# One transfer for three tiles of x, gamma first at the start, and a newly laid order of work, in an RMSNorm + QKV product on one core

## The chip, the core and the metric

The kernel runs on one core of a Trainium2 chip. A core has TensorE (PE, matrix products into PSUM), VectorE (DVE), ScalarE (ACT) and GpSimd (POOL, which doesn't touch PSUM here), and SyncE (SP), which here issues all transfers but that of gamma. The metric is the time of one execution on the device, in microseconds (us). Before the change the median of three runs is 361.82 us (358.01 to 362.8).

## The reference

```
batch, n_heads, seq, head_dim = 8, 12, 1024, 64       # dim = 768
x: (8, 1024, 768) float32; gamma: (768,); w_qkv: (768, 2304) float32
rms = np.sqrt(np.mean(x ** 2, axis=-1, keepdims=True) + eps)
x_norm = x / rms * gamma
return np.matmul(x_norm, w_qkv).astype(np.float32)    # (8, 1024, 2304)
```

x is 8192 rows of 768, which is 64 tiles of 128 rows. The result has 2304 columns.

## The kernel before, in words

**Tiles.** The columns of the result are halved, c = 0 and 1, 1152 columns each (HW), and each half has three blocks of 384 columns (CW). The depth of 768 is six slices of 128 (KO), halved into three and three (H). gamma is multiplied into the weights once (conv, into w_b), and the row's 1/rms is multiplied into x or into the result.

**Head.** The first 7 tiles of x (N_HEAD) are computed plainly while the weights still arrive: load_x, cast to bf16, tr (six transposes on TensorE), cp out of PSUM, then mm, one matmul of 128 x 384 for each depth slice (L517 to L521). evac multiplies by 1/rms on the way out of PSUM, store_h stores.

**Triples.** The other 57 tiles go in 19 groups of three, g = 0 to 18. Three tiles by two depth halves, times two depth halves by three column blocks, would be 18 block products; the kernel does it in 15 by sums and differences of blocks. For the weights these sums are made once per half (quad scales a block to f16 by a bound on it, bsum adds; 15 + 3 forms). For x they are made in each triple by osum (11 sums, nearly all on GpSimd). The tables A_OF, B_OF and CHAIN say which sums are multiplied (L361 to L364), and the 15 products accumulate in two PSUM banks (chains 0 and 1) whose value is read between the products. A triple passes through these steps:

- load_t (L577): one tile of x from HBM into one third of a buffer XI (three buffers); one DMA for each tile, 393 KB
- pstat (L582), prms (L585) on ScalarE: sum of squares of each tile, then the square root for three; precip (L588) on VectorE: the reciprocals
- pcast (L591): the tile times 1/rms, to f16
- pxbar (L601): the three tiles turned by one DMA transpose
- osum (L615): the 11 sums
- product (L619): three matmuls of 128 x 384 each, 0.163 us apart; 15 for each half of the columns
- hold (L632): the first value of a result block, moved from PSUM to the output buffer times a scale, on ScalarE
- join (L635): the further values, added to or subtracted from what lies in an output buffer, on VectorE
- pstore (L639): a finished 128 x 1152 piece to HBM, 590 KB. There are 14 output buffers (OUT): 8 of their own, and 6 that lie in w_b once the weights are used up (the profile names those w_b). An argument at the end of hold is the buffer that is taken.

**Order.** The order of the work is written out by hand in the string PLAN: items "name engine arguments" apart by ";", run through once in that order. Each engine does its items strictly in their order, and so does SyncE with its DMAs; an item waits for the data and buffers that it needs, and what stands behind it on the same engine waits too. So a DMA whose data isn't ready holds up all later DMAs. The products of two halves, and of neighbouring triples, are interleaved so that TensorE has work while one chain's value is read.

**Start.** TensorE first runs 14 matmuls on zeros (idle, L479). Then come the transposes of the first tile and of gamma (gamma_tr, L483), and behind the cast of the third tile VectorE copies gamma out of PSUM (gamma_cp, L487), for which the conversion of the weights waits.

Of the kernel before, what the change touches and what calls it, by code (L numbers as in the profile page):

```python
# [10 lines left out]
load_x SP 0 0;load_w SP 0 0 6;load_x SP 1;load_w SP 0 1 7;idle PE 14 512 0;load_x SP 2;load_w SP 0 2 8;load_w SP 0 3 9;  # L11
cast ACT 0 0;load_w SP 0 4 10;stat ACT 0;load_w SP 0 5 11;recip DVE 0;cast ACT 1;load_x SP 3 1;stat ACT 1;load_x SP 4;
tr PE 0 1;gamma_tr PE 2;recip DVE 1;cp ACT 0 0;tr PE 1 3;load_x SP 5;cast DVE 2;gamma_cp DVE;stat ACT 2;tr PE 2 4;cp DVE 1;
conv POOL 0 0 0 1;load_w SP 1 0 12;conv DVE 0 0 1 3;conv POOL 0 1 0 3;mm PE 0 0 0 5;mm PE 1 0 0 6;cp ACT 2;conv DVE 0 2 0 3;
mm PE 0 1 0 7;mm PE 1 1 0 1;mm PE 0 2 0 2;load_w SP 1 1 13;mm PE 1 2 0 3;mm PE 2 0 0 4;conv ACT 0 3 0 3;mm PE 0 0 1;
mm PE 1 0 1;mm PE 2 0 1;mm PE 0 1 1;load_w SP 1 2 6;mm PE 1 1 1;recip DVE 2;mm PE 0 2 1;bound ACT 0 0;bound DVE 0 1;
mm PE 1 2 1;conv POOL 0 4 0 3;mm PE 0 0 2;mm PE 1 0 2;mm PE 2 0 2;mm PE 0 1 2;mm PE 1 1 2;mm PE 0 2 2;load_w SP 1 3 7;
bound ACT 0 2;mm PE 1 2 2;mm PE 0 0 3;mm PE 1 0 3;conv DVE 0 5 0 3;mm PE 2 0 3;mm PE 0 1 3;mm PE 1 1 3;mm PE 0 2 3;
mm PE 1 2 3;bound ACT 0 3;bound DVE 0 4;mm PE 0 0 4;load_w SP 1 4 8;mm PE 1 0 4;mm PE 2 0 4;mm PE 0 1 4;mm PE 1 1 4;
mm PE 0 2 4;mm PE 1 2 4;mm PE 0 0 5;bound ACT 0 5;cast DVE 3 1;mm PE 1 0 5;mm PE 2 0 5;load_w SP 1 5 9;mm PE 0 1 5;  # L20
mm PE 1 1 5;evac DVE 0 0 10;mm PE 0 2 5;mm PE 1 2 5;evac ACT 1 0 11;cast DVE 4;mm PE 2 1 0 5;mm PE 2 1 1;mm PE 2 1 2;
load_x SP 6 2;evac ACT 0 1;fold DVE 0;mm PE 2 1 3;evac DVE 1 1;mm PE 2 1 4;bound_tr PE 0 6;conv POOL 1 0 0 3;mm PE 2 1 5;
evac ACT 0 2;tr PE 3 7;bound_top DVE 0;load_t SP 0 0 0;evac DVE 1 2;stat ACT 3;mm PE 2 2 0 1;mm PE 2 2 1;mm PE 2 2 2;
cp DVE 3 1;mm PE 2 2 3;conv POOL 1 1 0 3;mm PE 2 2 4;mm PE 2 2 5;tr PE 4 6;evac DVE 2 0 12;stat ACT 4;mm PE 3 0 0 2;
mm PE 3 0 1;recip DVE 3;mm PE 3 0 2;evac DVE 2 1;mm PE 3 0 3;conv POOL 1 2 0 3;mm PE 3 0 4;mm PE 3 0 5;evac DVE 2 2;cp ACT 4;
mm PE 3 1 0 3;mm PE 3 1 1;mm PE 3 1 2;mm PE 3 1 3;evac DVE 3 0 13;mm PE 3 1 4;mm PE 3 1 5;cast ACT 5;mm PE 3 2 0 7;
conv POOL 1 3 0 3;mm PE 3 2 1;recip DVE 4;mm PE 3 2 2;evac DVE 3 1;mm PE 3 2 3;store_h SP 0 0;mm PE 3 2 4;stat ACT 5;
mm PE 3 2 5;mm PE 4 0 0 4;bound DVE 1 0;mm PE 4 0 1;mm PE 4 0 2;mm PE 4 0 3;conv POOL 1 4 0 3;mm PE 4 0 4;mm PE 4 0 5;
evac ACT 3 2;bound_all PE 0 5;load_t SP 1 0 1;mm PE 4 1 0 1;evac DVE 4 0 6;mm PE 4 1 1;mm PE 4 1 2;bound ACT 1 1;mm PE 4 1 3;
tr PE 5 6;scales DVE 0;conv POOL 1 5 0 3;store_h SP 1 0;mm PE 4 1 4;recip DVE 5;mm PE 4 1 5;cp DVE 5;mm PE 4 2 0 2;  # L30
bound ACT 1 2;mm PE 4 2 1;mm PE 4 2 2;mm PE 4 2 3;evac DVE 4 1;quad POOL 0 0 0;mm PE 4 2 4;mm PE 4 2 5;store_h SP 2 0;
mm PE 5 0 0 3;mm PE 5 0 1;bound DVE 1 3;mm PE 5 0 2;load_t SP 0 1;pstat ACT 0 0;mm PE 5 0 3;mm PE 5 0 4;load_t SP 0 2;
mm PE 5 0 5;quad POOL 0 1 1;mm PE 5 1 0 7;mm PE 5 1 1;mm PE 5 1 2;evac ACT 4 2;mm PE 5 1 3;bound DVE 1 4;mm PE 5 1 4;
mm PE 5 1 5;bound ACT 1 5;mm PE 5 2 0 4;quad POOL 0 5 2;mm PE 5 2 1;mm PE 5 2 2;mm PE 5 2 3;mm PE 5 2 4;load_t SP 1 1;
mm PE 5 2 5;evac DVE 5 0 7;mm PE 0 3 0 5;mm PE 0 3 1;load_t SP 1 2;pstat ACT 1 0;mm PE 0 3 2;quad POOL 0 3 3;mm PE 0 3 3;
fold DVE 1;mm PE 0 3 4;evac DVE 5 1;mm PE 0 3 5;mm PE 1 3 0 6;mm PE 1 3 1;evac ACT 5 2;evac DVE 0 3 8;mm PE 1 3 2;
bound_tr PE 1 1;quad POOL 0 4 4;mm PE 1 3 3;quad ACT 0 2 5;mm PE 1 3 4;bsum DVE 0 15 add 0 1 6;mm PE 1 3 5;mm PE 2 3 0 2;
store_h SP 3 0;mm PE 2 3 1;mm PE 2 3 2;mm PE 2 3 3;mm PE 2 3 4;evac ACT 1 3 9;mm PE 2 3 5;mm PE 3 3 0 3;mm PE 3 3 1;
mm PE 3 3 2;evac ACT 2 3 10;bsum DVE 0 17 add 5 15 7;mm PE 3 3 3;store_h SP 4 0;mm PE 3 3 4;mm PE 3 3 5;pstat ACT 0 1;
mm PE 4 3 0 7;bound_top DVE 1;mm PE 4 3 1;mm PE 4 3 2;bsum DVE 0 14 sub 0 17 8;mm PE 4 3 3;mm PE 4 3 4;mm PE 4 3 5;  # L40
pstat ACT 0 2;mm PE 5 3 0 4;store_h SP 5 0;mm PE 5 3 1;evac DVE 3 3 11;mm PE 5 3 2;mm PE 5 3 3;mm PE 5 3 4;evac DVE 4 3 12;
mm PE 5 3 5;prms ACT 0;mm PE 0 4 0 5;mm PE 0 4 1;pstat ACT 1 1;mm PE 0 4 2;precip DVE 0;mm PE 0 4 3;bsum DVE 0 16 add 3 5 9;
mm PE 0 4 4;mm PE 0 4 5;mm PE 1 4 0 6;mm PE 1 4 1;pcast ACT 0 0 0;mm PE 1 4 2;bsum DVE 0 11 sub 14 3 10;mm PE 1 4 3;
mm PE 1 4 4;mm PE 1 4 5;mm PE 2 4 0 2;evac DVE 5 3 13;pstat ACT 1 2;mm PE 2 4 1;mm PE 2 4 2;mm PE 2 4 3;mm PE 2 4 4;
pcast DVE 0 1;mm PE 2 4 5;mm PE 3 4 0 1;pcast ACT 0 2;mm PE 3 4 1;mm PE 3 4 2;bsum DVE 0 7 add 4 5 11;mm PE 3 4 3;mm PE 3 4 4;
bound_all PE 1 3;mm PE 3 4 5;prms ACT 1;pxbar SP 0 0 3 2;bsum DVE 0 9 sub 5 2 12;mm PE 4 4 0 7;mm PE 4 4 1;evac ACT 0 4;
mm PE 4 4 2;mm PE 4 4 3;mm PE 4 4 4;precip DVE 1;evac ACT 1 4;mm PE 4 4 5;bsum DVE 0 10 add 3 7 13;mm PE 5 4 0 4;mm PE 5 4 1;
mm PE 5 4 2;pcast ACT 1 0 1;mm PE 5 4 3;bsum DVE 0 13 sub 9 17 14;mm PE 5 4 4;mm PE 5 4 5;mm PE 0 5 0 5;mm PE 0 5 1;
evac ACT 2 4;mm PE 0 5 2;pcast DVE 1 1;mm PE 0 5 3;mm PE 0 5 4;mm PE 0 5 5;pcast ACT 1 2;mm PE 1 5 0 6;load_t SP 2 0 0;
bsum DVE 0 6 sub 1 4 15;mm PE 1 5 1;mm PE 1 5 2;mm PE 1 5 3;mm PE 1 5 4;bsum DVE 0 8 add 1 2 16;evac ACT 3 4;mm PE 1 5 5;  # L50
mm PE 2 5 0 2;mm PE 2 5 1;mm PE 2 5 2;evac ACT 4 4;mm PE 2 5 3;bsum DVE 0 12 sub 17 10 17;mm PE 2 5 4;mm PE 2 5 5;
evac ACT 5 4;mm PE 3 5 0 1;pxbar SP 1 0 3 0;mm PE 3 5 1;osum DVE 0 6 add 1 5 0;mm PE 3 5 2;mm PE 3 5 3;evac ACT 0 5;
mm PE 3 5 4;osum DVE 0 11 sub 2 4 1;mm PE 3 5 5;mm PE 4 5 0 7;osum DVE 0 12 add 0 6 2;evac ACT 1 5;mm PE 4 5 1;mm PE 4 5 2;
osum DVE 0 13 sub 11 6 3;mm PE 4 5 3;mm PE 4 5 4;cast ACT 6 0;osum DVE 0 7 add 1 3 4;mm PE 4 5 5;product PE 0 0 10 4;
osum DVE 0 8 add 4 12 5;mm PE 5 5 0 5;osum DVE 0 9 add 7 13 6;evac ACT 2 5;product PE 0 0 2 6;osum DVE 0 15 add 0 1 7;
store_h SP 0 1;hold ACT 0 0 10 8 1 6;mm PE 5 5 1;osum DVE 0 14 add 2 3 8;tr PE 6 2;store_h SP 1 1;osum DVE 0 16 sub 4 14 9;
hold ACT 0 0 2 2 -1 7;product PE 0 0 3;store_h SP 2 1;osum DVE 0 10 add 0 2 10;evac ACT 3 5;mm PE 5 5 2;
bsum DVE 0 18 sub 13 11 18;product PE 0 0 12;evac ACT 4 5;mm PE 5 5 3;store_h SP 3 1;osum POOL 1 6 add 1 5 11;
osum DVE 1 11 sub 2 4 12;mm PE 5 5 4;mm PE 5 5 5;hold ACT 0 0 12 0 1;osum POOL 1 7 add 1 3 13;cp ACT 6 1;product PE 0 0 7;
osum DVE 1 12 add 0 6 14;store_h SP 4 1;hold ACT 0 0 3 4 -1 8;mm PE 6 0 0 1;mm PE 6 0 1;mm PE 6 0 2;  # L60
osum POOL 1 13 sub 11 6 15;stat ACT 6;mm PE 6 0 3;product PE 0 0 11;join DVE 0 0 7 6 -1 8 -1;mm PE 6 0 4;mm PE 6 0 5;
scales DVE 1;product PE 0 0 6;osum POOL 1 8 add 4 12 16;hold ACT 0 0 11 3 1;osum DVE 1 9 add 7 13 17;product PE 1 0 10 7;
hold ACT 0 0 6 7 1;product PE 0 0 13;osum POOL 1 15 add 0 1 18;hold ACT 1 0 10 8 1 9;osum DVE 1 14 add 2 3 19;
product PE 1 0 2 2;load_t SP 2 1;product PE 0 0 0;quad ACT 1 0 19;quad POOL 1 1 20;product PE 1 0 3;load_t SP 2 2;
join DVE 0 0 13 6 1 6 1;mm PE 6 1 0 3;mm PE 6 1 1;hold ACT 1 0 2 2 -1 10;mm PE 6 1 2;join DVE 0 0 0 1 -1 2 -1;
product PE 0 0 9;load_t SP 3 0 1;hold ACT 1 0 3 4 -1 11;quad POOL 1 5 21;osum DVE 1 16 sub 4 14 20;product PE 1 0 12;
join DVE 0 0 9 8 -1 8 1;evac ACT 5 5;product PE 0 0 1;bsum DVE 1 15 add 0 1 22;product PE 1 0 11;hold ACT 1 0 12 0 1;
# [305 lines left out]
def kernel(  # L373
# [199 lines left out]
    def rows(v, g, i):  # L573
        r0 = P * (N_HEAD + 3 * g + i)
        return v[r0:r0 + P, :]

    def load_t(eng, g, i, *slot):  # L577
        if slot:
            xi[g] = XI[slot[0]]
        nc.sync.dma_start(out=xi[g][:, i], in_=rows(xf, g, i))  # L580
# [104 lines left out]
```

## Time and profile before

| | |
|---|---|
| median of three runs | 361.82 us |
| profiled execution, its time | 363.96 us |
| profiled execution, span of its instructions | 362.2 us |
| mean granted TensorE clock | 0.987 |
| busy: PE, ACT, DVE, POOL | 336.2, 259.4, 247.8, 193.5 us |
| DMA moved | 119.36 MB, mean 330 GB/s |
| loads of x (L469, L580) | 64 of 384 KB, 6.5 us median from issue to landing |
| stores (L529, L640) | 128 of 576 KB, 5.5 us median (82 from ot), 5.6 us (46 from w_b) |
| transposes by DMA (L602) | 19, 7.1 us median |

In a group of instructions the page shows line, engine, operation, tiles and shapes, the count, then busy time in all, mean ns of one, and the idle time just before them with what ended most of it. In the list of waits the three numbers are us in total, how often, and the longest. In the chain and the timelines the first number is the start and the second the duration, in us. In the tables by window come the busy time and count of each engine, the granted clock, the DMA share and GB/s. KB here are 1024 bytes; MB and GB are powers of ten.

### The profile page before, as it was taken

Reading aid. Unit: us, or ns where it says so; the run is one execution under the profiler, and the core shown is the slowest. Engines: PE = TensorE matmul, PEld = TensorE weight load, DVE = VectorE, ACT = ScalarE, POOL = GpSimd, SP = SyncE. Lnnn points to the kernel's source line nnn. Section 1 sums busy time; section 2 is a strip of 40 time slices with the busy share of each in tenths; the row PEclk is TensorE's granted clock in tenths of the full one; section 3 lists DMA queues with packets and bytes.
Section 4 is the critical chain, followed back from the end, with each engine's and each line's share of the span. In section 5 each row is a group of like instructions: output and inputs, shape, how many; then the busy total and the mean of one; then the engine's idle time right before and its main releaser. Section 6 shows DMA issues by size and latency. Waiting matters only on the chain.

```text
span 362.2 us, 6131 instructions
## 1 busy us (share of the span) xinstructions
PE 336.2 (93%) x2023; PEld 196.5 (54%) x2023; DVE 247.8 (68%) x456; ACT 259.4 (72%) x491; POOL 193.5 (53%) x218
## 2 busy tenths in 40 slices
PE   6799999998999799999999797999998989999993
PEld 2465556554654356556655464666565655656651
DVE  0799978897666467666866466676676666767764
ACT  5898989798975688568885665973987838854440
POOL 0359029008399735960938937099109974099100
PEclk9899999999999899999999999999999999999998
DMA  8999899999999999999999999999999999997466
GB/s 284 413 408 414 278 257 368 405 340 358 277 265 370 340 340 286 342 368 329 359 321 317 359 306 391 311 325 370 410 208 366 356 307 388 280 350 300 196 273 250
DMA packets 73804, 119.36 MB, mean 330 GB/s; under 512 B 47654, under 2 KB 47660, under 8 KB 73772
## 3 DMA queue, kind: packets, MB, share of 16 engines
q1 hardware_dynamic: 73760, 118.96, 99.2%
q8 instruction: 16, 0.26, 0.3%
q14 instruction: 16, 0.13, 0.1%
q10 hardware_dynamic: 12, 0.00, 0.0%
HBM read 32.25 MB, written 75.50 MB: 297 GB/s over the span
## 4 chain that ended last, share of the span: by engine, by line
PE 63%; DMA 18%; issue 5%; DVE 4%; ACT 4%; POOL 2%; SPq 2%; DVEq 0%; ACTq 0%; POOLq 0%
PE ps L624 52%; DMA xi<-in_x_dram 14%; PE ps L520 11%; DVE ot L636 3%; DMA xt<-xb 2%; POOL su L460 2%; ACT junk L583 2%; ACT ot L450 1%; DMA out_dram<-ot 1%; SPq L640 1%; DVE w_b L636 1%; PE ps L509 0%; DVE wh L460 0%; ACT w_b L450 0%; SPq L580 0%
## 5 line engine op out<-in xcount | busy, mean ns | idle before, releaser
L624 PE MATMUL ps<-wh,su 128*128 128x384 f16 x1254 | 229.8, 327 | 15.1 <-ACT ot L450 6.3
L624 PEld LDWEIGHTS <-su 128*128 128x128 f16 x1254 | 122.5, 98 | 101.5 <-issue 15.9
L460 POOL TENSOR_TENSOR su<-xt 128x384 f16<-128x384 f16 x106 | 96.2, 923 | 123.7 <-DMA xt<-xb 54.9
L636 DVE SCALAR_TENSOR_TENSOR ot<-ps,sc,ot 128x384 f32<-128x384 f32 x204 | 119.8, 613 | 53.7 <-PE ps L624 50.0
L636 DVE SCALAR_TENSOR_TENSOR w_b<-ps,sc,w_b 128x384 f32<-128x384 f32 x138 | 81.4, 613 | 36.0 <-PE ps L624 35.5
L450 ACT ACTIVATE ot<-ps,sc 128x384 f32<-128x384 f32 x136 | 75.6, 579 | 37.5 <-PE ps L624 36.3
L624 PE MATMUL ps<-wh,xt 128*128 128x384 f16 x456 | 95.8, 327 | 0.9 <-DVE ot L636 0.8
L583 ACT ACTIVATE junk<-xi 128x768 bf16<-128x768 f32 x57 | 47.9, 840 | 28.9 <-DMA xi<-in_x_dram 28.4
L450 ACT ACTIVATE w_b<-ps,sc 128x384 f32<-128x384 f32 x92 | 51.7, 578 | 19.7 <-PE ps L624 19.0
L624 PEld LDWEIGHTS <-xt 128*128 128x128 f16 x456 | 44.6, 98 | 31.5 <-issue 2.5
L450 ACT ACTIVATE xb<-xi,st 128x768 f16<-128x768 f32 x55 | 50.3, 928 | 0.8 <-DVE st L589 0.8
L460 POOL TENSOR_TENSOR su<-xt,su 128x384 f16<-128x384 f16 x52 | 47.6, 915 | 1.3
L520 PE MATMUL ps<-w_b,xt 128*128 128x384 bf16 x252 | 46.6, 334 | 0.3 <-POOL w_b L457 0.2
L520 PEld LDWEIGHTS <-xt 128*128 128x128 bf16 x252 | 24.7, 100 | 17.3 <-issue 1.9
L460 POOL TENSOR_TENSOR su<-su,su 128x384 f16<-128x384 f16 x35 | 32.2, 919 | 0.0
L457 POOL TENSOR_SCALAR w_b<-ot,g_sb 128x1152 bf16<-128x1152 f32 (+1 forms) x9 | 10.7, 1190 | 17.2 <-DVE g_sb L488 9.3
L460 DVE TENSOR_TENSOR wh<-wh,wh 128x1152 f16<-128x1152 f16 x26 | 19.7, 788 | 0.1
L450 ACT ACTIVATE ot<-ps,rs 128x384 f32<-128x384 f32 x26 | 13.6, 575 | 0.0
L457 POOL TENSOR_SCALAR wh<-w_b,sc 128x1152 f16<-128x1152 bf16 x9 | 11.6, 1308 | 0.0
L583 ACT ACTIVATION_READ_ACCUMULATOR junk<-xi 128x1 f32 x57 | 10.9, 191 | 0.0
L455 DVE TENSOR_SCALAR ot<-ps,rs 128x384 f32<-128x384 f32 x16 | 9.5, 607 | 0.9 <-DMA out_dram<-ot 0.6
L542 ACT ACTIVATE junk<-w_b 128x1152 bf16<-128x1152 bf16 x7 | 8.1, 1157 | 0.7 <-DVE w_b L455 0.6
(47 smaller groups left out, 73.8 us busy)
## 6 DMA issues: line engine op xcount, KB each, us to landing
out_dram<-ot SPq DMA_DIRECT2D x82, 576.0 KB, 5.5
out_dram<-w_b SPq DMA_DIRECT2D x46, 576.0 KB, 5.6
xi<-in_x_dram SPq DMA_DIRECT2D x64, 384.0 KB, 6.5
ot<-in_w_qkv_dram SPq DMA_DIRECT2D x12, 576.0 KB, 10.0
xt<-xb SPq DMA_TRANSPOSE x19, 7.1
g<-in_gamma_dram ACTq DMA_DIRECT2D x1, 3.0 KB
```

The costliest lines, as they stand in the source:

```text
L450: nc.scalar.activation(out=out, in_=in_, func=AF.Copy, scale=scale, bias=0.0)
L455: nc.vector.tensor_scalar(out=out, in0=in_, scalar1=scale, scalar2=None, op0=mult)
L457: nc.gpsimd.tensor_scalar(out=out, in0=in_, scalar1=scale, scalar2=1.0, op0=mult, op1=mult)
L460: (nc.vector if eng == "DVE" else nc.gpsimd).tensor_tensor(out=out, in0=in0, in1=in1, op=op)
L520: nc.tensor.matmul(out=po["p", t, w], lhsT=head_xt(t)[:, k, :], rhs=w_b[:, k // H, w, k % H], start=(k == 0), stop=(k == KO - 1))
L542: nc.scalar.activation(out=junk, in_=v, func=AF.Abs, accum_out=o)
L583: nc.scalar.activation(out=junk[:, :K], in_=xi[g][:, i], func=AF.Square, accum_out=ST[g % 6][:, i:i + 1])
L624: nc.tensor.matmul(out=o, lhsT=a[:, k, :], rhs=b[:, k, :], start=(r in FIRST and k == 0), stop=(k == H - 1), skip_group_check=True)
L636: nc.vector.scalar_tensor_tensor(out=part(g, c, i, slot), in0=po[g, c, CHAIN[r]], scalar=(sc if sign > 0 else nsc)[c], in1=part(g, c, j), ...
L640: nc.sync.dma_start(out=rows(of, g, i)[:, HW * c:HW * (c + 1)], in_=ot[g, c, i])
```

## The change

load_t takes a triple in one DMA (1180 KB in thousands of bytes) instead of three. At the start the transpose of gamma comes first on TensorE, 9 zero matmuls follow it, and VectorE copies gamma ahead of the casts. PLAN is laid anew: the same products, joins and transposes in another order. 59 of the 228 holds move from ScalarE to VectorE; both casts of triples that VectorE had go to ScalarE, two bounds from ScalarE to VectorE, one quad from ScalarE to GpSimd, one osum from VectorE to GpSimd, two evacs from VectorE to ScalarE, one cp from ScalarE to VectorE. The stores stand later behind their joins and in ascending order of tiles.

```
-    def rows(v, g, i):
-        r0 = P * (N_HEAD + 3 * g + i)
-        return v[r0:r0 + P, :]
-
-    def load_t(eng, g, i, *slot):
-        if slot:
-            xi[g] = XI[slot[0]]
-        nc.sync.dma_start(out=xi[g][:, i], in_=rows(xf, g, i))
+    def load_t(eng, g, slot):
+        xi[g] = XI[slot]
+        r0 = P * (N_HEAD + 3 * g)
+        nc.sync.dma_start(out=xi[g], in_=xf[r0:r0 + 3 * P, :].rearrange("(i p) k -> p i k", p=P))
...
     def pstore(eng, g, c, i):
-        nc.sync.dma_start(out=rows(of, g, i)[:, HW * c:HW * (c + 1)], in_=ot[g, c, i])
+        r0 = P * (N_HEAD + 3 * g + i)
+        nc.sync.dma_start(out=of[r0:r0 + P, HW * c:HW * (c + 1)], in_=ot[g, c, i])
```

PLAN at the start:

```
-load_x SP 0 0;load_w SP 0 0 6;load_x SP 1;load_w SP 0 1 7;idle PE 14 512 0;load_x SP 2;load_w SP 0 2 8;load_w SP 0 3 9;
-cast ACT 0 0;load_w SP 0 4 10;stat ACT 0;load_w SP 0 5 11;recip DVE 0;cast ACT 1;load_x SP 3 1;stat ACT 1;load_x SP 4;
-tr PE 0 1;gamma_tr PE 2;recip DVE 1;cp ACT 0 0;tr PE 1 3;load_x SP 5;cast DVE 2;gamma_cp DVE;stat ACT 2;tr PE 2 4;cp DVE 1;
-conv POOL 0 0 0 1;load_w SP 1 0 12;conv DVE 0 0 1 3;conv POOL 0 1 0 3;mm PE 0 0 0 5;mm PE 1 0 0 6;cp ACT 2;conv DVE 0 2 0 3;
...
+load_x SP 0 0;load_w SP 0 0 6;load_x SP 1;load_w SP 0 1 7;load_x SP 2;load_w SP 0 2 8;load_w SP 0 3 9;cast ACT 0 0;
+load_w SP 0 4 10;gamma_tr PE 0;idle PE 9 512 1;stat ACT 0;gamma_cp DVE;load_w SP 0 5 11;conv DVE 0 0 0 1;conv POOL 0 0 1 3;
+recip DVE 0;cast ACT 1;load_x SP 3 1;stat ACT 1;load_x SP 4;conv DVE 0 1 0 3;tr PE 0 2;tr PE 1 3;load_x SP 5;cp ACT 0 0;
+recip DVE 1;cast DVE 2;load_w SP 1 0 12;stat ACT 2;tr PE 2 4;cp DVE 1;mm PE 0 0 0 5;mm PE 0 1 0 6;cp DVE 2;conv POOL 0 2 0 3;
```

The order of DMAs on SyncE around triple 13, before (other items left out):

```
load_t 13 0; pstore 9 1 1; load_t 13 1; pstore 9 1 0; pstore 10 0 2; load_t 13 2; load_t 14 0; pstore 10 0 1; pxbar 12;
pstore 10 0 0; pstore 10 1 2; pstore 10 1 1; pstore 10 1 0; pxbar 13; pstore 11 0 2; pstore 11 0 1; pstore 11 0 0
```

and after:

```
load_t 13; pstore 8 1 2; pxbar 12; pstore 9 0 0; pstore 9 0 1; pstore 9 0 2; pstore 9 1 0; pstore 9 1 1; load_t 14;
pstore 9 1 2; pxbar 13; pstore 10 0 0; pstore 10 0 1; pstore 10 0 2; pstore 10 1 0; pstore 10 1 1; load_t 15
```

## The prediction

> **What bounds the kernel now.** I read the page first, then the TensorE waits, the chain that ended last, the places of DMA issues in the program, and DMA in windows of 1 us.
>
> ```profile
> span 362.2 us, 6131 instructions
> PE 336.2 (93%) x2023; PEld 196.5 (54%) x2023; DVE 247.8 (68%) x456; ACT 259.4 (72%) x491; POOL 193.5 (53%) x218
> DMA packets 73804, 119.36 MB, mean 330 GB/s; under 512 B 47654, under 2 KB 47660, under 8 KB 73772
> PE 63%; DMA 18%; issue 5%; DVE 4%; ACT 4%; POOL 2%; SPq 2%; DVEq 0%; ACTq 0%; POOLq 0%
> L583 ACT ACTIVATE junk<-xi 128x768 bf16<-128x768 f32 x57 | 47.9, 840 | 28.9 <-DMA xi<-in_x_dram 28.4
> ```
>
> TensorE is busy for 93% of the span, so little can be won: what it waits for. ScalarE stands 28.4 us before the statistics of rows (L583), for loads of x.
>
> ```profile
> PE ps L624 <- ACT ot L450: 6.3, 8, 2.4
> PE ps L624 <- POOL su L460: 4.4, 7, 1.0
> PE ps L624 <- ACT w_b L450: 3.5, 2, 2.3
> PE ps L624 <- DVE ot L636: 1.4, 5, 0.4
> PE ps L520 <- POOL w_b L457: 0.2, 1, 0.2
> ```
>
> After the first matrix product (11.4 us) these waits make 15.8 us. The chain tells whose fault ACT's 9.8 are:
>
> ```profile
> 110.65 1.04 SPq L580
> 111.69 0.05 issue
> 111.74 6.51 DMA xi<-in_x_dram
> 118.34 0.94 ACT junk L583 x2
> 119.33 0.18 issue
> 119.51 0.57 ACT ot L450
> 120.12 27.71 PE ps L624 x159
> ```
>
> One tile is issued at 110.65 and lands 6.5 us later; the statistics queued for it on ScalarE hold back the move out of PSUM queued behind them, and TensorE stands. This shape comes back at 151.9, 176.6, 197.4, 217.5, 247.6 and 291.4. The plan explains it: load_t 13 0 stands 7 products ahead of pstat 13 0, 7 x 3 matmuls x 0.163 us = 3.4 us, while the loads' line shows (least, median, most):
>
> ```profile
> DMA to landing us min/median/max: 3.4/6.4/11.3
> ```
>
> **The second limit is DMA.** From 50 to 320 us it moved 338 GB/s, 91.3 MB in 270 us. Plain transfers run at some 408 GB/s. Transposes do not:
>
> ```profile
> 92.00:93.00 1.00, 1.00 (x8) 0.61 (x7) 0.00 (x0) 1.00 (x3) 0.50 (x1) 1.00 0.98 376
> 93.00:94.00 1.00, 1.00 (x8) 0.59 (x7) 0.17 (x1) 1.00 (x3) 0.00 (x0) 1.00 3.64 166
> 94.00:95.00 1.00, 1.00 (x8) 0.59 (x6) 0.90 (x2) 0.94 (x2) 0.00 (x0) 1.00 0.28 31
> 95.00:96.00 1.00, 1.00 (x9) 0.59 (x7) 0.17 (x1) 1.00 (x3) 0.00 (x0) 1.00 0.15 39
> 98.00:99.00 1.00, 1.00 (x8) 0.61 (x7) 0.94 (x2) 0.37 (x1) 0.70 (x1) 1.00 1.08 442
> ```
>
> ```profile
> 89.33 6.78 SPq L602 DMA_TRANSPOSE xt<-xb  x1
> ```
>
> The last column of the windows is GB/s, the one before it the DMA share. The second fence is from SyncE's queue, start and duration: it issues nothing else from 89.33 to 96.11, and DMA runs dry before it is done. Over the transposes from 133 us on, what is missing to 405 GB/s in the 8 us or so behind each issue is 2.2 us on average (1.1 to 4.2). With its own 0.59 MB (1.45 us) one costs 3.65 us of DMA. A ceiling: the 270 us less 81.3 MB at 408 GB/s leave 71 us for 17 transposes, 4.2 us each, holes included.
>
> **What stays.** 1962 matmuls of 384 columns (252 of the head, 570 x 3) x 0.163 us = 319.8; transposes and bounds behind the first product 1.9; before it 11.4; behind the last matmul 5.1. Sum 338.2 of 362.2. The other 24.0: the 15.8 of waits; half clock at 11.8 to 15 us and at 121 to 125 us, 1.7 us each; 4.8 of restarts (some 24 waits, each losing the 0.17 us by which two products otherwise overlap).
>
> **The change, part by part.**
>
> *Start.* The gamma transpose moves ahead, 9 warm-up matmuls follow it instead of 14 before it (5.15 us for 14 is 0.37 each, 3.3 us). Gamma lands at a time that the trace doesn't show: not before 3.7 (x's first tile, issued with it) nor after 6.2 (the transpose ran unheld). So the warm-up ends between 7 and 9.6 us. The first product waits for the third tile anyway: it landed at 10.0, cast 0.56, transposed 0.34, and the weights' conversion (10.74, 0.6) goes out of that path: -0.4. Against it, a full conversion of weight block 1 stands ahead of that cast on VectorE (two conversions, of 768 and 1152 columns, took 2.04 us together, so some 1.2): up to +0.8. I take 0.
>
> *The clock.* TensorE idled 2.1 and 1.6 us around 8.5 us, and its granted clock was half until 15. The Trainium skill (TensorE: Matmul & The Clock Gate, Part 1: The HAM clock gate) lets the clock drop only after an idle window of about 3.4 us; with warm-up that ends later this would not happen, and the sum would be 1.7 us less. The row shows a drop behind shorter gaps. I keep the 1.7; its ends are 0 (no drop) and 2.5 (half as long again).
>
> *One transfer for a triple.* 57 loads become 19; the bytes are the same. SyncE's issues fall from 223 to 185; a tile's issue took 0.33 to 1.7 us (median 0.91), and the triple has three times the rows, so I count 1.0 to 2.7 and no gain. The price: the first tile's statistics wait for the third tile. Landing: 6.4 + 0.79 MB / 0.408 = 8.3 us. Queued behind the wait on ScalarE stand the holds of the running products, and TensorE waits for them. But the new plan places load_t 13 15 products ahead of pstat 13 0, 7.3 us (6.8 to 8.3 in triples 6 to 18), where it was 7 (3.4). It also puts only stores ahead of it whose joins ended long before, so SyncE can issue it early. I take 2 us left over the run of the 9.8 of waits, their restarts (1.7) and the clock loss at 121 us (1.7): 0 to 9.
>
> The Trainium skill (DMA: Bandwidth & Descriptors, Anatomy of one DMA — SWDGE (gpsimd) path) speaks against the merger: the semaphore moves only once the last byte has landed. It also gives about 2.0 us + bytes / 436 GB/s for another way of issuing; worked out from that as an estimate, a triple lands in 4.7 us and no statistics would ever wait, 2 us less in the sum.
>
> *Transposes.* Issue of pxbar to the first sum on GpSimd: 10 to 17 products before (4.9 to 8.3 us), 13 to 15 now for most (6.4 to 7.3), against 7.1 us to land. From the last sum to the first product there are 5 us more. GpSimd's 4.4 plus restarts 1.2 fall to 2 (0.5 to 5).
>
> *59 holds from ScalarE to VectorE*, 0.607 us each by the row of L455 instead of 0.579: VectorE +36 us over the run, 284 of some 340; per triple 18 joins x 0.613 + 3 holds x 0.607 = 12.9 of 14.7 us. ScalarE falls by 34 us. TensorE waited 1.4 us for VectorE's joins; fuller, I take 2 with restarts (1 to 5). If ScalarE's relief were not there, these holds would stand behind the statistics as before.
>
> *Stores.* pstore now stands 5 to 18 us behind its join and SyncE seldom waits for VectorE. In return output buffers come back late: a store stood at least 17 us ahead of the next writer of its buffer (after the head); now 9 products, 4.4 us, in the tightest place, and a store takes 5.5 us to land. hold 16 0 10 needs pstore 13 1 1. Ahead of that landing lie 32.2 MB of loads, 97 stores x 0.59 MB = 57.2 MB, 18 transposes: 89.4 / 0.408 = 219 + 18 x 3.65 = 66 + 2.6 until data flow + 2 of startup holes + 2 to land = 291.5. The plan wants it after 276 us of TensorE work, at 287. So DMA itself delays the new plan by 4.5; I take 5, with 1 to 15 (4.2 us a transpose gives 10 more). The same sum at the last transpose: before 313 against 305, and it really landed some 12 later still (issued at 319.5), because SyncE stood in waits (65.7 us for VectorE's joins alone) with loads behind them; now 305 against 302.
>
> **Sum.** 338.2 + clock 1.7 + loads 2 + sums 2 + VectorE 2 + DMA 5 = 350.9 of span. The profiled execution took 364.0 beside its 362.2, and the median of the runs, 361.8, lies 2.1 below it: 350.9 + 1.8 - 2.1 = 350.6, about **350.5**.
>
> **Rivals.**
> *DMA keeps its pace* (same): transposes at 4.2 us, so a delay of 15 instead of 5 on the way to that buffer: 360.5. For it: DMA share about 1.0 in nearly every window. Against: the end has room, 330 to 360 us at 0.6 to 0.7, into which the new plan moves six stores.
> *Buffers come late* (at the edge of 2%): stores land 5.5 us after issue where 4.4 to 4.9 are given, in triples 13 to 16: one more us at each of five returns, 355.5. Against: a store whose join is old can be issued early.
> *The triple lands late* (slower): if it takes the longest time seen for a tile plus the two others, 11.3 + 1.9 = 13.2 us, against 7.3, ScalarE stands 5.9 x 17 triples = 100 us. TensorE lost 9.8 of ScalarE's 28.4, 0.35: 35 us instead of 2, 383.5. It is slower than before by 2% (369) from a loss of 20.5 us on: 20.5 / 0.35 / 17 triples = 3.4 us, so where the landing passes 10.7 us. For it: the completion for all three, on the queue behind five stores. Against: the median 6.4.
> *The re-laid start doesn't work* (no warm clock, later first product): +1.5, inside the forecast's range.
>
> **Chances.** Forecast 0.60 (own range 342 to 356), DMA's pace 0.17, late buffers 0.10, late triple 0.13. Faster by over 2% (below 354.6, about what a measurement can tell from no change): nine tenths of the forecast and half of the late buffers, 0.60; slower all of the late triple and some of DMA's pace, 0.16; the rest 0.24. The range 342 to 364 leaves out most of the late triple and a little below.
>
> **What would show it.** ACT's wait for x below 10 us of 28.4; a triple landing in 7 to 10 us; no chain piece "DMA xi" over 5 us; TensorE's waits below 9; VectorE busy at 280 to 285, ScalarE near 225; GB/s above 345; first product at 11 to 12 us. Waits of holds or evacuations for "DMA out_dram" would speak for the late buffers, ACT waits over 60 us for the late triple. Wrong is the forecast if the span is above 357 or if the waits for x fall and the time doesn't.

## The result and the profile after

The changed kernel takes 358.44 us (median of 20 runs, 356.39 to 360.53) beside 361.76 for the kernel before (20 runs, 357.25 to 364.85): a ratio of 0.994, 95% interval 0.9911 to 0.9969. That is a gain of 0.6%, where 3.1% was forecast. The ratio leaves out the runs that lie over 1.5% above the fastest of their kernel (five of the kernel before, whose profiled execution of 363.96 us lies as high). The profiled execution of the changed kernel took 359.0 us, 357.1 of it in the span.

First the page of the changed kernel: the span, busy times, DMA, the shares of the chain by engine and by line, and the group of the statistics of rows.

```profile
span 357.1 us, 5991 instructions
PE 334.3 (94%) x2018; PEld 197.0 (55%) x2018; DVE 280.5 (79%) x513; ACT 230.7 (65%) x430; POOL 194.5 (54%) x220
DMA packets 73195, 119.35 MB, mean 334 GB/s; under 512 B 47046, under 2 KB 47052, under 8 KB 73164
PE 48%; DMA 29%; ACT 9%; SPq 5%; issue 4%; DVE 3%; POOL 2%; DVEq 0%; ACTq 0%
L572 ACT ACTIVATE junk<-xi 128x768 bf16<-128x768 f32 x57 | 47.9, 840 | 21.5 <-DMA xi<-in_x_dram 21.0
```

Work moved from ScalarE to VectorE as meant. But ScalarE still stands 21.0 us for x (28.4 before), DMA is no faster (334 GB/s beside 330), and its share of the chain rose from 18% to 29%. The view of TensorE's waits, behind the first product (us in total, times, longest):

```profile
PE ps L613 <- ACT ot L443: 4.9, 7, 1.5
PE ps L613 <- ACT w_b L443: 4.1, 4, 2.5
PE ps L613 <- DVE su L453: 0.9, 1, 0.9
PE ps L613 <- DVE w_b L625: 0.8, 3, 0.4
```

The waits for GpSimd's sums (4.4 before) are gone. Those for ScalarE are 9.0 and were 9.8: that is most of the disappointment, in two lines. The chain that ended last shows where they come from (start, duration):

```profile
148.06 0.04 issue
148.11 10.15 DMA xi<-in_x_dram
158.26 0.02 issue
158.28 0.02 ACT junk L572
158.31 0.73 issue
159.03 0.19 ACT junk L572
159.22 0.48 ACT w_b L443
159.69 0.04 issue
159.74 16.27 PE ps L613 x99
```

It is the shape that the kernel before had, with a 10 us transfer in the place of a 6.5 us one: load, statistics, the move out of PSUM queued behind them, TensorE. It comes back six times between 178.07 and 256.20 us, each time with a transfer of 8.3 to 10.3 us. SyncE's timeline shows why the load is not issued sooner:

```profile
138.46 4.92 SPq L591 DMA_TRANSPOSE xt<-xb  x1
143.43 0.57 SPq L630 DMA_DIRECT2D out_dram<-w_b  x1
144.05 0.43 SPq L630 DMA_DIRECT2D out_dram<-ot  x1
144.58 3.49 SPq L630 DMA_DIRECT2D out_dram<-w_b  x3
148.11 1.24 SPq L569 DMA_DIRECT2D xi<-in_x_dram  x1
149.53 1.10 SPq L630 DMA_DIRECT2D out_dram<-w_b  x1
153.84 5.93 SPq L591 DMA_TRANSPOSE xt<-xb  x1
```

A transpose holds SyncE for 4.9 us, five stores take 4.7 us more, and only then is the load issued. Ahead of the transpose SyncE waits for the buffer that it writes into (the triple three before has to be done with it), as the list of SyncE's waits says:

```profile
SPq L591 <- PE ps L613: 52.8, 17, 5.4
SPq L591 <- POOL su L453: 35.3, 13, 6.0
```

So the load cannot be early: it hangs on TensorE through the transpose ahead of it, and TensorE hangs on it through ScalarE. It is a loop, and it can be measured. For the 12 transposes from 105 us on that have a load behind them, the timelines of SyncE and ScalarE give, on average, 10.2 us from the start of the transpose to the issue of the load, and 9.25 us from there to the first statistics. In PLAN the products between the same two pairs of items make 9.9 and 7.5 us (0.163 us a matmul, mean of the same 12 triples). The second stretch is 1.75 us short on average. The first fits, but not because the products set it: SyncE issues in it with hardly a gap, 5.6 us for the transpose and the rest for three to five stores. Where the load stands two stores further up (below), PLAN has 7.7 us for this stretch, and it still takes 9.9.

### The profile page after: what moved, and what is told of

It reads as the page before. It is cut to its first block, busy times and chain, and to the rows that moved or that the text cites. A ratio compares the mean times of both kernels' runs of the same rounds, so it can differ in the third digit from the quotient of the medians.

```text
span 357.1 us, 5991 instructions
## 1 busy us (share of the span) xinstructions
PE 334.3 (94%) x2018; PEld 197.0 (55%) x2018; DVE 280.5 (79%) x513; ACT 230.7 (65%) x430; POOL 194.5 (54%) x220
## 4 chain that ended last, share of the span: by engine, by line
PE 48%; DMA 29%; ACT 9%; SPq 5%; issue 4%; DVE 3%; POOL 2%; DVEq 0%; ACTq 0%
PE ps L613 42%; DMA xi<-in_x_dram 23%; PE ps L513 5%; ACT junk L572 4%; SPq L630 4%; DMA out_dram<-ot 3%; ACT ot L443 3%; POOL su L453 2%; DMA ot<-in_w_qkv_dram 2%; DVE w_b L625 2%; ACT xb L443 1%; DVE ot L625 1%; ACT w_b L443 1%; PE ps L502 0%; DVE w_b L448 0%
## 5 line engine op out<-in xcount | busy, mean ns | idle before, releaser
L613 PE MATMUL ps<-wh,su 128*128 128x384 f16 x1254 | 225.9, 327 | 10.8 <-ACT ot L443 4.9
L613 PE MATMUL ps<-wh,xt 128*128 128x384 f16 x456 | 93.2, 329 | 0.5 <-DVE w_b L625 0.4
L443 ACT ACTIVATE ot<-ps,sc 128x384 f32<-128x384 f32 x105 | 59.2, 578 | 52.7 <-PE ps L613 50.1
L572 ACT ACTIVATE junk<-xi 128x768 bf16<-128x768 f32 x57 | 47.9, 840 | 21.5 <-DMA xi<-in_x_dram 21.0
L443 ACT ACTIVATE w_b<-ps,sc 128x384 f32<-128x384 f32 x64 | 36.1, 576 | 33.4 <-PE ps L613 32.9
L513 PE MATMUL ps<-w_b,xt 128*128 128x384 bf16 x252 | 47.8, 339 | 0.0
L453 POOL TENSOR_TENSOR su<-xt,su 128x384 f16<-128x384 f16 x51 | 46.6, 913 | 0.0
L448 DVE TENSOR_SCALAR ot<-ps,sc 128x384 f32<-128x384 f32 x31 | 19.1, 615 | 8.5 <-PE ps L613 8.3
L448 DVE TENSOR_SCALAR w_b<-ps,sc 128x384 f32<-128x384 f32 x28 | 17.2, 613 | 5.6 <-PE ps L613 5.3
L450 POOL TENSOR_SCALAR w_b<-ot,g_sb 128x1152 bf16<-128x1152 f32 (+1 forms) x9 | 11.1, 1239 | 16.4 <-DMA ot<-in_w_qkv_dram 16.4
L443 ACT ACTIVATE ot<-ps,rs 128x384 f32<-128x384 f32 x28 | 14.6, 582 | 1.4 <-PE ps L513 1.4
L450 POOL TENSOR_SCALAR wh<-w_b,sc 128x1152 f16<-128x1152 bf16 x10 | 12.7, 1284 | 0.0
```

Of the source, the lines that this page charges most:

```text
L443: nc.scalar.activation(out=out, in_=in_, func=AF.Copy, scale=scale, bias=0.0)
L448: nc.vector.tensor_scalar(out=out, in0=in_, scalar1=scale, scalar2=None, op0=mult)
L450: nc.gpsimd.tensor_scalar(out=out, in0=in_, scalar1=scale, scalar2=1.0, op0=mult, op1=mult)
L453: (nc.vector if eng == "DVE" else nc.gpsimd).tensor_tensor(out=out, in0=in0, in1=in1, op=op)
L513: nc.tensor.matmul(out=po["p", t, w], lhsT=head_xt(t)[:, k, :], rhs=w_b[:, k // H, w, k % H], start=(k == 0), stop=(k == KO - 1))
L572: nc.scalar.activation(out=junk[:, :K], in_=xi[g][:, i], func=AF.Square, accum_out=ST[g % 6][:, i:i + 1])
```

## The experiments

Each ratio is to the kernel before on the same chip, with its 95% interval. Between chips the kernel before moved by 3 us (361.25 to 364.25), so times are best compared within one set.

### Three transfers again, in the new order

```
-load_t SP 13 2
+load_t SP 13 0 2;load_t SP 13 1;load_t SP 13 2
```

> The changed kernel with its one transfer for a triple taken apart again into three, at the same place in the order. 'Order on the queue': the first tile lands at most 1.9 us (two tiles of 0.39 MB at 408 GB/s) sooner, the last one when it did; ScalarE's waits for x fall from 21 to some 12, 355-358.5. Rival 'merger': the late landing of the first tile is what ate the gain, so all of it comes back: 349-353.

Measured: 352.66 us, ratio 0.9703 (0.963 to 0.9776). Repeated on another chip, beside the changed kernel itself as control:

> The changed kernel itself, on the same chip as the next three: all theories 357-360 (ratio 0.994).

> The new order with three transfers in place, first tile first, on the same chip as the merged kernel: 351-354 in both theories, TensorE's waits for ScalarE half of the merged kernel's 9.0.

Measured: 358.82 us (0.9916, 0.9886 to 0.9947) for the changed kernel and **351.81 us (0.9725, 0.9687 to 0.9762)** with three transfers, the fastest of that set. TensorE's waits for ScalarE in the control:

```profile
PE ps L620 <- ACT ot L450: 6.5, 8, 1.5
PE ps L620 <- ACT w_b L450: 5.0, 4, 2.2
```

The page of the kernel with three transfers and its waits:

```profile
PE 332.8 (95%) x2018; PEld 196.6 (56%) x2018; DVE 280.3 (80%) x513; ACT 232.4 (66%) x430; POOL 194.5 (56%) x220
DMA packets 73805, 119.37 MB, mean 341 GB/s; under 512 B 47654, under 2 KB 47660, under 8 KB 73772
PE 71%; DMA 12%; DVE 4%; SPq 4%; POOL 3%; issue 2%; ACT 1%; DVEq 0%; ACTq 0%
```

```profile
PE ps L627 <- ACT ot L456: 2.1, 4, 1.4
PE ps L627 <- ACT w_b L456: 0.8, 2, 0.5
```

The chain is TensorE's again, its waits for ScalarE are 2.9 us where the control has 11.5, and the first statistics begin 6.9 us after the first load is issued. So the new order is worth 2.75%, and the one transfer gives 7.0 us of it back. (The page's GB/s is the bytes over the span: with the same bytes it rises because the span is shorter, and is no evidence of its own.)

### The merger alone, in the old order

```
-load_t SP 13 0 2;...;load_t SP 13 1;...;load_t SP 13 2
+load_t SP 13 2
```

> The kernel before, with only the merger: one transfer for a triple at the place where its first tile was loaded, all else in the old order. 'Order on the queue': second and third tiles come earlier, the first 1.9 us later, and the waits for x stay near 28 us: 359-365. 'Merger': each triple's first tile is late in an order laid for single tiles, the waits for x grow beyond 45 us: 366-374.

Measured: 381.21 us, ratio 1.0507 (1.0406 to 1.0607), above both ranges. The one transfer stands where the first tile's stood. TensorE's waits for ScalarE in this kernel:

```profile
PE ps L624 <- ACT ot L450: 13.6, 8, 4.4
PE ps L624 <- ACT w_b L450: 7.9, 2, 4.9
```

By itself the merger is a loss of 5%: TensorE waits 21.5 us for ScalarE where it was 9.8, and the granted clock costs 10.2 us where it was 3.4 (the sum of what windows of 1 us lack to full clock). The new order hides most of that.

### Is it the big transfer, or the tile that comes last?

With three transfers the first statistics need one tile. Here the third tile is loaded first, so that they need all three, as with the merged transfer:

```
-load_t SP 13 0 2;load_t SP 13 1;load_t SP 13 2
+load_t SP 13 2 2;load_t SP 13 1;load_t SP 13 0
```

> The triple's load in three transfers at the same place in the new order, as in the split kernel (352.7), but issued third tile, second, first. Theory 'first tile': what the merger costs is that the statistics of the first tile, and the holds queued behind them on ScalarE, wait for the last byte of 1.18 MB; with the first tile landing last they wait again, 356.5-360. Rival 'the big transfer itself': one DMA of 1.18 MB moves or lands worse than three, or fills the queue otherwise; then three transfers are good in any order, 351-354.

Measured: 355.35 us, 0.9804 (0.9711 to 0.9898); too wide to tell. Again in the set of the control (358.82; three in order 351.81), with a mixed form, first tile alone and the other two in one transfer:

> The new order with three transfers in place, third tile first, on the same chip as the merged and the split kernel. Theory 'first tile' (only the landing of the first tile counts): the same as the merged kernel within 0.5%, 356-359. Rival 'the big transfer itself': the same as the split kernel, 351.5-354. If both count, between: near 355.

> The new order, the first tile of a triple in a transfer of its own, the second and third in one of 0.79 MB behind it. 'First tile': the same as the split kernel, 351.5-354.5, since the first statistics start as early and last 1 us while the others come. 'The big transfer itself': two thirds of the merger remain, 355-357.5.

Measured: 353.65 us, 0.9784 (0.9742 to 0.9825), reversed; 356.05 us, 0.9843 (0.9803 to 0.9883), one and two. Having to wait for all three tiles costs 1.8 us (351.81 to 353.65, intervals that overlap). The other 5.2 us come with the one transfer in the place of three. How they arise these runs do not show. In this set the first statistics begin 9.4 us after the issue of the one transfer and 9.0 after that of the first of three, and paid in a dozen triples 0.44 us would be 5.3. But the earlier executions of the same two kernels have 9.25 and 9.34, the other way round, and the two profiled executions of this set lie 2.9 us apart (358.16 and 355.29) and not 5.2. With one and two, the second statistics wait in place of the first: ScalarE is idle for 1.1 us before them and for 0.2 before the first (means of the 12 triples).

### More lead for the load

If the load is late, issue it earlier. It was moved directly behind the transpose ahead of it, and ahead of that transpose, in triples 5 to 18:

```
-pxbar 12; pstore 9 0 0; pstore 9 0 1; pstore 9 0 2; pstore 9 1 0; pstore 9 1 1; load_t 14; pstore 9 1 2; pxbar 13
+pxbar 12; load_t 14; pstore 9 0 0; pstore 9 0 1; ...                   (behind)
+load_t 14; pxbar 12; pstore 9 0 0; pstore 9 0 1; ...                   (ahead)
```

> In the changed kernel, load_t of triples 5 to 18 is moved on SyncE's queue from behind about five stores to directly behind the transpose ahead of them. Theory 'order on the queue': the load comes late because the transpose ahead of it waits until TensorE and GpSimd have read the transpose buffer's last triple, holds the queue for 5.8 us, and five stores of up to 1.2 us each go first; moved, a load is issued some 5 us sooner and lands without those stores ahead, ScalarE's 21.0 us of waits for x fall below 6, TensorE's 9.0 behind ScalarE below 3, and the time falls from 358.4 to 348-353. Rival 'throughput': DMA already moves what it can, the stores now come 3 us later and holds wait for output buffers instead; 357-361.

> As the kernel with the load behind the transpose, but the load of triples 5 to 18 stands one place further up, ahead of that transpose, so that it doesn't wait for the transpose buffer either. 'Order on the queue': no wait for x is left at all (below 2 us), but the transpose now queues behind 1.18 MB (2.9 us at 408 GB/s) in every triple, so GpSimd's sums come later; 347-354. 'Throughput': 357-361, with waits for GpSimd's sums or output buffers.

Measured: 372.49 us, 1.0245 (1.0163 to 1.0327), behind; 359.22 us, 0.9894 (0.9821 to 0.9967), ahead. ScalarE's wait for x fell to 2.1 and 1.0 us of 21, and the time did not fall: ahead it is in the rival's range, behind it is above both. VectorE's waits in the second:

```profile
DVE w_b L455 <- DMA out_dram<-w_b: 5.3, 2, 3.8
DVE ot L455 <- DMA out_dram<-ot: 2.6, 3, 1.3
```

The five stores are now late in the place of the load, and the first values of result blocks wait for their output buffers (ScalarE another 6.9 us). With the load behind the transpose those waits are 28.2 us in all, and the mean granted clock is 0.969 where it was 0.982. A smaller step, two stores up (so that the load mostly stands behind the third store; the 359.2 us of the expectation below are those of the load ahead of the transpose):

```
-pxbar 12; pstore 9 0 0; pstore 9 0 1; pstore 9 0 2; pstore 9 1 0; pstore 9 1 1; load_t 14; pstore 9 1 2; pxbar 13
+pxbar 12; pstore 9 0 0; pstore 9 0 1; pstore 9 0 2; load_t 14; pstore 9 1 0; pstore 9 1 1; pstore 9 1 2; pxbar 13
```

> The changed kernel with one edit: of triples 5 to 18, the load stands two stores earlier on SyncE's queue, behind the second store after the transpose and not behind the fifth or so; some 2.2 us earlier at 1.1 us an issue. If the loss is the lead (the stretch from the transpose to the statistics, 20 us where the plan has 18), ScalarE's wait for x falls below 8 of 22.7, TensorE's waits for ScalarE from 11 to 3 or 4, and the time to 351 to 354. If DMA's pace or the output buffers set the time, the waits turn up at out_dram (stores landing late), as when the loads stood three stores further up (359.2), and the time stays at 356 or more.

Measured: 364.92 us, 1.0124 (1.0069 to 1.018): slower than the kernel before. The waits turned up at out_dram, but that alone was to cost less. SyncE's timeline of this kernel:

```profile
137.13 9.01 SPq L600 DMA_TRANSPOSE xt<-xb  x1
146.19 0.57 SPq L639 DMA_DIRECT2D out_dram<-w_b  x1
146.81 0.43 SPq L639 DMA_DIRECT2D out_dram<-ot  x1
147.34 0.96 SPq L639 DMA_DIRECT2D out_dram<-w_b  x1
148.34 1.24 SPq L578 DMA_DIRECT2D xi<-in_x_dram  x1
149.63 2.54 SPq L639 DMA_DIRECT2D out_dram<-w_b  x3
153.77 8.87 SPq L600 DMA_TRANSPOSE xt<-xb  x1
```

Two stores fewer stand between the transpose and the load, and yet the load is issued 11 us behind the transpose's start (9.9 on average, 10.1 in the control). The transpose itself holds SyncE for 9 us here: three stores were issued just ahead of it, and it seems to leave the queue only as they drain. The lead that the place gave (2 us) was handed back by the transpose, and the stores behind it are late for their buffers (22 us of waits for out_dram).

The other way to lead is a later reader: statistics, square root and reciprocal of triples 6 to 18 four products later.

```
-load_t SP 13 2; (15 products); pstat ACT 13 0
+load_t SP 13 2; (19 products); pstat ACT 13 0
```

> The changed kernel, merged load and all, with the three statistics, their root and reciprocal of triples 6 to 18 moved 4 products (2.0 us) later in the order, so that the holds of those products stand ahead of the wait for x on ScalarE. 'First tile': the wait for x falls from 21 us to below 8 and TensorE's waits for ScalarE from 9.0 to below 5; 352-355.5. 'The big transfer itself' (DMA loses time as such): 357-360, the waits turn up behind the transposes instead.

Measured: 357.99 us, 0.9872 (0.9785 to 0.9958): no change from the changed kernel that the intervals show. ScalarE's wait for x fell from 21 to 14.7 us, TensorE's for ScalarE stayed at 9.4. The casts, the transpose and the next load then come later too, so the loop is not shortened: from the start of a transpose to the end of the third statistics of the load behind it there are 23.0 us, 22.7 in the control below.

### The store between the load and the next transpose

In the changed kernel mostly one store stands there (two or three ahead of the transposes of triples 5, 6 and 11, none ahead of those of 9, 14 and 17). It goes behind the transpose:

```
-load_t 14; pstore 9 1 2; pxbar 13; pstore 10 0 0
+load_t 14; pxbar 13; pstore 9 1 2; pstore 10 0 0
```

> The changed kernel with one edit: of triples 5 to 18, the one store that stands between the load of a triple and the next transpose moves behind that transpose, so that nothing follows the load on the queue but the transpose. If the triple's transfer lands late because the store issued 0.1 us behind it shares the DMA engines with it (590 KB), its landing falls by a part of the store's 1.45 us, from 9.4 to 8.4 or so, ScalarE's wait for x from 22.7 to under 15, and the time goes from 358.8 to 353 to 355. If it lands late for itself, or behind what was issued before it, the landing stays above 9 us and the time at 357 to 360.

Measured: 354.18 us, 0.983 (0.9784 to 0.9877). The time is what sharing with that store was to give, but the reason is only partly right: the first statistics begin 9.1 us after the load's issue, 0.3 earlier and not 1, and ScalarE still waits 16.1 us for x. What changed more is the transpose, 3.7 us on SyncE on average from 105 us on, where it was 5.7. SyncE's timeline:

```profile
146.20 1.18 SPq L577 DMA_DIRECT2D xi<-in_x_dram  x1
152.13 3.75 SPq L599 DMA_TRANSPOSE xt<-xb  x1
155.98 0.53 SPq L638 DMA_DIRECT2D out_dram<-w_b  x1
```

Does the one transfer still cost anything then? Three kernels on one chip, all with that store moved: three transfers in order, three reversed, and the merged one again.

> New order, three transfers in the place of the one, and the store of triples 5 to 18 that stands between the load and the next transpose moved behind that transpose. If the stretch from transpose to first statistics sets the time (17.6 us with three transfers, 19.5 merged, 18.8 merged with the store moved), it is shorter again, some 17, and the time is 348 to 350. If DMA's pace or the holds set it from 351 on, it stays at 350.5 to 353.5, and the waits are those for out_dram.

> The same with the third tile first, so that the first statistics wait for all three tiles as with the merged transfer. If the store behind the load made the big transfer 5 us dearer than three in reversed order (358.8 against 353.65), the two are now equal within 1.5 us: 352 to 354 beside 354.2 for the merged one. If the big transfer is dearer in itself, 350 or less.

> The kernel with one transfer for the triple and that store moved, once more as the control on the same chip: 353 to 355.5, transposes that hold SyncE for 3.7 us each.

Measured: 352.58 us (0.9688, 0.9648 to 0.9728), 352.83 us (0.9696, 0.9658 to 0.9733), 354.22 us (0.9745, 0.9703 to 0.9786). Merged and reversed are now 1.4 us apart, with intervals that overlap, where they were 5.2. So most of the merged transfer's price hung on the store between it and the next transpose. Three in order gain nothing from the move that the intervals show (0.9725 without it, 0.9688 with it). There the waits for output buffers make 12.3 us and those for x 8.7, so some 352 seems to be where this loop no longer decides. The loop, from the timelines (means over 12 triples from 105 us on, us):

| kernel | transpose holds SyncE | its start to load's issue | issue to first statistics | sum | start to end of third statistics | time |
|---|---|---|---|---|---|---|
| one transfer (control) | 5.7 | 10.1 | 9.4 | 19.5 | 22.7 | 358.82 |
| three, reversed | 5.7 | 10.1 | 9.0 | 19.1 | 22.3 | 353.65 |
| three, in order | 6.3 | 10.7 | 6.9 | 17.6 | 21.0 | 351.81 |
| first tile, then two in one | 6.4 | 10.9 | 7.1 | 18.0 | 22.4 | 356.05 |
| one, two stores up | 7.9 | 9.9 | 10.2 | 20.1 | 23.7 | 364.92 |
| one, store moved | 3.7 | 9.7 | 9.1 | 18.8 | 21.9 | 354.18 |
| three reversed, store moved | 3.6 | 9.6 | 9.2 | 18.8 | 21.9 | 352.83 |
| three in order, store moved | 4.8 | 10.7 | 7.1 | 17.8 | 21.2 | 352.58 |

Up to the first statistics the sum does not order the times: the mixed form has 18.0 and takes 356.05 us. Up to the end of the third, for which the square root and so the casts and the next transpose wait, the stretch nearly does: 21.0 and 21.2 go with some 352 us, 21.9 with 353 and 354, 22.3 to 22.7 with 354 to 359, 23.7 with 365. A second execution of the same kernel differs here by 0.1 to 0.3 us, so the step between two neighbouring rows proves nothing, and that the stretch sets the time is read from this order, not tested by itself. Whether the 0.3 us of the load or the 2 us of the transpose did it was not separated; most of the latter is given back within the stretch, because the moved store now lies in it: five or six stores and their gaps take 6 us behind the shorter transpose, where three to five took 4.4 behind the longer.

### The holds that moved to VectorE

The new order with three transfers, and the 59 holds back on ScalarE:

```
-hold DVE 0 0 11 3 1
+hold ACT 0 0 11 3 1
```

> The new order with three transfers in place of the one (351.8), and with the 59 holds that the change moved to VectorE back on ScalarE. If the moved holds carry the gain of the new order (they don't stand behind the statistics), TensorE waits 8 us or more for ScalarE, and the time is 357 to 361. If the gain is the places of the loads and stores, ScalarE's 34 us more (265 of 350) are covered, VectorE falls to 245, and the time is 350 to 353.

Measured: 354.22 us, 0.9824 (0.978 to 0.9868). That lies between the two expectations. Of the 2.75% the holds carry about 1 (0.9725 against 0.9824, on two chips), the rest of the new order what is left. TensorE's waits for ScalarE rise from 2.9 to 7.1 us.

### What stands below 351

Half of the stored bytes of the triples: this kernel writes only the left half of each 128 x 1152 piece, 33.6 MB less, and leaves the rest of the result unwritten.

```
-out=of[r0:r0 + P, HW * c:HW * (c + 1)], in_=ot[g, c, i]
+out=of[r0:r0 + P, HW * c:HW * c + HW // 2], in_=ot[g, c, i][:, :HW // 2]
```

> The changed kernel with every store of the triples cut to the left half of its columns, so half of the triples' result is not written: 33.6 MB less to move, number and order of all DMAs unchanged. If DMA's pace sets the time in any part, landings get shorter by the stores ahead in the queue and the waits for x vanish: 343-349, about TensorE's own work of 338 plus the start. If the waits come from the order alone (the transpose behind its buffer's reader), 354-358.

Measured: 345.84 us (two runs), 0.9544 (0.9446 to 0.9641), with the one transfer. ScalarE's wait for x is 1.2 us, stores land in 3.0 us. One window from 50 to 320 us, first of this kernel, then of the changed one (each engine's busy time and count; last the granted clock, DMA share, GB/s):

```profile
50.00:320.00 270.00, 267.37 (x1647) 160.35 (x1646) 227.81 (x416) 183.83 (x341) 175.40 (x198) 1.00 0.80 240
```

```profile
50.00:320.00 270.00, 260.67 (x1584) 154.91 (x1583) 221.25 (x404) 179.37 (x335) 168.98 (x191) 0.99 1.06 333
```

With DMA at 0.8 the same plan runs 63 matmuls further in these 270 us: 10.3 us. With room on DMA, the loop closes in time with the one transfer too: the transposes hold SyncE for 3.1 us (5.3 in the control, over the whole kernel), the stores are issued faster, and the load is issued 5.8 us behind the start of the transpose ahead of it, where it was 10.2. What is late in the changed kernel is late with DMA full.

Last the clock at the start, three transfers and 3 + 5 more zero matmuls in the gaps:

```
-tr PE 0 2;tr PE 1 3;...;tr PE 2 4
+tr PE 0 2;idle PE 3 512 1;tr PE 1 3;...;idle PE 5 512 1;tr PE 2 4
```

> The split kernel (352.7) with 3 more zero matmuls between the first two transposes of the start and 5 between the second and the third, in TensorE's idle time of 1.0 and 2.0 us there. If those idle times bring the clock down to half behind 9 us, the loss (about 1.7 us in that kernel's profile) goes: 350.5-352. If the drop has another cause: 352-354, or later by up to 1 if the third transpose has to wait for them.

Measured: 353.79 us, 0.9747 (0.9666 to 0.9827), beside 352.66 and 0.9703 without them, on another chip. The clock, changed kernel first, then this one (granted clock third from the end):

```profile
10.00:12.00 2.00, 1.30 (x9) 0.97 (x10) 1.55 (x5) 1.09 (x3) 0.72 (x1) 0.50 1.01 415
12.00:14.00 2.00, 2.00 (x8) 0.99 (x7) 1.54 (x3) 1.43 (x3) 1.73 (x2) 0.50 1.01 414
```

```profile
10.00:12.00 2.00, 1.32 (x12) 0.94 (x13) 1.72 (x6) 0.88 (x3) 0.89 (x1) 1.00 1.00 408
12.00:14.00 2.00, 2.00 (x15) 1.22 (x13) 1.45 (x2) 1.60 (x3) 1.55 (x2) 1.00 1.04 426
```

The half clock of the start is gone, and no gain is seen; with intervals of some 0.8% to either side, 1.7 us would not stand out. In the profiled executions the lead is lost soon: TensorE reaches its 21st matmul of 384 columns at 14.3 us instead of 15.8, but its 201st at 48.5 instead of 48.4, and the transpose of triple 2 starts at 76.1 us instead of 74.7.

## Why the prediction was wrong

The forecast was 350.5 us, 3.1% faster; 358.4 came, 0.6% faster. That lies in the wide range of 342 to 364, which covers rivals too, but outside the forecast's own, 342 to 356. The sum made 350.9 of span; the span was 357.1.

**The step that failed is the loads' 2 us.** Taken apart as the sum was, the span after has 9.0 us of waits for ScalarE, some 2 of restarts with them, and 1.7 of half clock behind the longest (269 to 272.4 us): 12.7 in the place of 2, hardly anything won beside the 13.2 of before (9.8, 1.7 and 1.7). (The control's execution has 11.5 us of these waits and no half clock there.) Within that step:

- The landing was nearly right: 8.6 us median where 8.3 was worked out (least, median, most, below); 9.25 on average to the first statistics from 105 us on, inside the 7 to 10 given.

```profile
DMA to landing us min/median/max: 6.5/8.6/12.9
```

- The lead in the plan, 7.3 us, was read rightly as well. It was already 1 us less than the landing; by the prediction's own rule (0.35 of ScalarE's wait, 17 triples) that alone is 6 us, and 2 were taken. The sentence that closed this gap is the one that failed: that SyncE could issue the load early, since the joins of the stores ahead of it were old. It looked at the stores and not at the transpose ahead of them. That waits 88.1 us in all for the last readers of its buffer (the two lines of L591), and then holds SyncE for 5.6 us, with three to five stores behind it before the load's turn comes. The load was never early.
- The rival "the triple lands late" had the right mechanism with too high a price: the longest landing of all, 35 us. Its rule, 0.35 of each us of ScalarE's wait in 17 triples, with the measured 9.4 and the plan's 7.3 gives 0.35 x 17 x 2.1 = 12.5 us. That this is near the 12.7 is luck. The rule counts TensorE's waits alone, which were 9.0; it makes ScalarE's wait 36 us, where 21.0 came; and TensorE lost 0.43 of that, not 0.35.
- The rival "DMA keeps its pace" is nearest in number (360.5). But with three transfers the same bytes and the same 19 transposes take 351.8 us, so its price of 4.2 us a transpose is not what set the time.

**The other terms.** Most held. First product at 11.32 us (11 to 12 given). VectorE 280.5 us busy (280 to 285), ScalarE 230.7 (near 225). TensorE's waits for VectorE 1.7 where 2 were taken (0.8 for joins, 0.9 for a sum of x); for GpSimd nothing where 2 were. The clock at the start cost 2.7 us from 11 us on, just past its end of 2.5. The bounds for gamma were wrong: it released its transpose at 3.1 us and not between 3.7 and 6.2, so the warm-up ended at 6.8 us, ahead of idle times of 1.0 and 2.0 us, and half clock followed until 16.4. The new order with three transfers, where the failed step is away, took 351.8 us, a span of 349.6 beside the sum's 350.9. So near a match is partly luck, as the sum has 2 us for GpSimd's sums and 5 for DMA, neither of which shows as such (TensorE's waits there are 2.9 us for ScalarE and 1.8 for VectorE).

**DMA** did 334 GB/s, not over 345, because the span stayed long with the same bytes. The 5 us for a late output buffer cannot be seen by themselves: ScalarE waited 2.1 us for output buffers, and what the span has left over is some 2. With the loads moved up those waits came, in the form of the rival "buffers come late" (28 and 15 us).

**The rule on large transfers.** The Trainium skill (DMA: Bandwidth & Descriptors, Rules for kernel authors) advises to coalesce small transfers and to make them 1 MiB or more for the highest bandwidth. Here 57 loads of 393 KB became 19 of 1180 KB, and the kernel with the smaller ones was faster, 351.8 us against 358.8. That does not test the rule's bandwidth, as the bytes are the same and the time is set by waits; it shows that size alone is not the goal. The sentence cited in the prediction, that the semaphore moves only once the last byte has landed, fits the trace: the first statistics began 9.4 us after the issue with the one transfer and 6.9 with three. But waiting for all three tiles cost 1.8 of the 7.0 us (the reversed order).

## What to carry to other kernels

Before a transfer is said to be early or late, follow its queue back to the last instruction that waits for the engine you want to feed: if there is one, the transfer's lead is fixed by that loop, however old the data of its neighbours is. Before you merge loads whose first part is needed first while DMA is full, price the longer landing against the lead in the plan, triple by triple; and if you merge, look at what is queued between the big one and the next transpose by DMA. When an edit removes a wait and the time stays, look for the same microseconds at the neighbours on the queue (here at the output buffers) before you look for a new cause.

## What the runs showed of the hardware

- A DMA transpose of 0.59 MB holds SyncE the longer, the more is in flight when it is issued: 3.1 us on average over the kernel with half stores, 3.7 with a gap of some 4 us ahead of it, 5.7 in the control, mostly behind one store, 7.9 behind three. Stores behind it wait that long. One kernel's trace shows it too: with the load directly behind the transpose, those issued 10 us or more behind the DMA before them took 2.5 to 3.4 us (4 of the transposes from triple 5 on), those with four or more transfers still in flight 7.1 to 8.8 (5). That it waits for the queue to drain is inferred from this.
- The granted clock can fall to half behind gaps shorter than the 3.4 us that the Trainium skill names (TensorE: Matmul & The Clock Gate, Part 1: The HAM clock gate): behind one of 2.53 us in the changed kernel. TensorE's timeline there, and the window that follows (third from the end, the clock):

```profile
267.91 2.01 PE L613 MATMUL ps<-wh,su 128*128 128x384 f16 x9 [2.53 <-ACT w_b L443]
```

```profile
270.00:272.00 2.00, 2.00 (x8) 0.95 (x7) 1.31 (x3) 0.30 (x2) 2.00 (x3) 0.50 0.99 406
```

In the middle of a kernel it did so behind gaps of 2.17, 2.32, 2.41 and 2.52 us too (three transfers reversed, in its first runs; load behind the transpose; kernel before; merger in the old order), but not behind one of 3.11 (merger in the old order, at 110.9 us) or 2.86 (load behind the transpose, at 302.1 us). So here the length of the gap alone does not decide.

- 38 more issues on SyncE cost nothing that can be seen: three issues took 3.3 us, the merged one 1.2, and the kernel with three was the faster.
